# Emission by a list scheduler with a time model in an eight-core decoder trunk

## The chip, the cores and the metric

The kernel runs on the eight cores of one Trainium2 chip (two dies: cores 0 to 3 and 4 to 7). Each core computes one sequence of the batch; the cores don't exchange data. The metric is the device time of the slowest core in microseconds (us). In the lines of the profile, PE is TensorE (PEld its weight loads), DVE is VectorE, ACT is ScalarE and POOL is GpSimd. A PSUM bank is one of the eight buffers of `ps_all` (128 x 8 x 512 in the kernel) that TensorE writes its results to; the program has it written again only when DVE or ACT has read it (gate/up stood 104 us for that in the kernel before). GLA is gated linear attention.

Executions come in two states. In the slow one the cores of a die, or of both, are granted a lower TensorE clock for long stretches. Even a fast run can hold a short stretch at 0.81 of the clock on some cores, so beside the time of a run I use its **undisturbed cores**: those whose clock records in the profiled run hold no 0.81 at all. Three chips served the experiments, called A, B and C here. Cores of the kernel before that ran at a mean clock of at least 0.944 had medians of 6857, 6849 and 6837 us on them, so up to 20 us between kernels can be the chip; where that matters, I say which chip it was.

## The reference

```python
# x: (8, 4096, 1024) float32.  D_MODEL 1024, D_FF 2816
def rms_norm(x, g):
    return x * rsqrt(mean(x * x, -1) + 1e-6) * g
def swiglu_ffn(h, w_in, w_down):
    gate, up = split(h @ w_in, 2)
    return (silu(gate) * up) @ w_down

for i in range(2):                     # layer 0: GLA, layer 1: differential attention
    x = x + 0.5 * swiglu_ffn(rms_norm(x, g), w_in, w_down)      # FFN 0 / FFN 2
    x = x + mixer[i](rms_norm(x, g))
    x = x + 0.5 * swiglu_ffn(rms_norm(x, g), w_in, w_down)      # FFN 1 / FFN 3
return rms_norm(x, final_norm)
# mixer 0: gated linear attention, chunks of 64, 4 heads (projection, "core", output projection)
# mixer 1: (softmax(Q1 K1^T) - lam * softmax(Q2 K2^T)) V, causal, 8 heads, two 64-wide maps each
# ... cut
```

A core works through eight tiles of 512 tokens; each passes all of both layers. Keys and values of earlier tiles are kept in device memory, so attention grows from tile 0 to tile 7.

## The kernel before

A program in Python writes out each engine's instructions in a fixed order; the engines then run in that order and wait on semaphores. The trace shows one order whatever the times: in the profiled run before, ACT's 3826 and DVE's 4435 records have the same sequence on all eight cores, and TensorE's 37152 on the six cores that hold that many. The kernel before decides the order with generators that yield a cost. Two of them, attention and a chain of dense tasks, are woven by how far each has come:

```python
db["list"] = [0, 1] if lim else [0, 1, 2, 3]          # PSUM banks of the dense work
gens = [[chain(x), 0.0, max(1e-6, sum(tk.cost for tk in x)), bool(x)] for x in (lt, dn)]
while any(g[3] for g in gens):
    live = [g for g in gens if g[3]]
    g = min(live, key=lambda g: g[1] / g[2])           # the one least far along
    try:
        g[1] += next(g[0])
    except StopIteration:
        g[3] = False
```

What follows a matmul group (evacuation, norm) is emitted at once. The norm that ends a projection holds its transposes back by one row block only:

```python
class NormPipe:
    # ... cut
    def done(self, s, of):             # after the x update of row block s, half `of`
        stat_half(p, s, of)            # ACT: square with row sums
        if of == 1:
            stat_rstd(p, s)            # POOL: 1/sqrt
            i = norm_hb(p, s)          # DVE: x * rstd, bf16
            self.pump()                # PE: transposes of the row block before
            self.pend = (p, s, i, self.n_idx)
# ... cut
```

The key tiles go through two staging buffers to device memory, and attention issues one chunk of scores at a time, the values two chunks behind:

```python
def k_cons(c, b):
    i = c % 2
    k.op(DVE, lambda: nc.vector.tensor_copy(out=kst[i][:], in_=bank[b][:]), ...)
    # ... cut
    k.dma(SP, t_kc[c, t], t_kst[i], [(kvc[c, t, :, 0:512], kst[i][:])])
# ... cut
for n in range(N + LAG):               # LAG = 2
    if n < N:
        qk(n)                          # 4 matmuls of 64 rows, two at once; then exp on ACT
    if n >= LAG:
        pv(n - LAG)                    # 8 matmuls of 128 rows x 129 columns
    # ... cut
```

The softmax here doesn't subtract the row's maximum and nothing guards it: scores larger than these inputs give would overflow.

## Time and profile before

| | before |
|---|---|
| time | 6953.8 us, median of three (6903.14 to 7202.15) |
| profiled run, slowest core | 7143.8 us, with one stretch of 2300 to 2600 us, most of it at clock 0.81, on every core |
| undisturbed execution, stitched from two cores | 6860 us |
| TensorE useful work at measured spacing | 5441 us |

The lines are in the prediction below. Two habits of reading matter: "busy" counts slow matmuls as busy, so useful work is columns times the measured spacing (0.2158 us for 512 columns; at full clock starts on core 2 are 0.109 us apart for 256 columns, 0.056 to 0.057 for 129 and 0.056 for 128, and 64-row matmuls that go two at once start 3 to 4 ns apart); and a wait listed as "PE L412 <- DVE L403" is time in which TensorE stood at a transpose until the DVE had written its input.

### The profile page before, as it was taken

What the parts mean: (1) busy time and instruction counts of PE and PEld (TensorE: products, weight loads), DVE (VectorE), ACT (ScalarE), POOL (GpSimd) and SP (SyncE); (2) the same over time, 40 slices, a digit from 0 to 9 for tenths busy, and PEclk for the clock granted to TensorE, in tenths of its full rate; (3) what the DMA queues carried; (4) which work ended last, traced back from release to release, by engine and by line L of the source; (5) the groups of instructions that cost most, each with busy time, mean ns of one, the idle gap of its engine ahead of it and who ended that gap; (6) DMA issues with size and microseconds to landing.
All of it is one profiled execution on the core that took longest, in us unless ns stands there. A gap on an engine that the chain in (4) does not pass through costs nothing.

```text
span 7143.8 us, 103951 instructions; the slowest of 8 cores (7062.5 to 7143.8 us)
## 1 busy us (share of the span) xinstructions
PE 6330.8 (89%) x37152; PEld 2987.2 (42%) x37152; DVE 2530.7 (35%) x4435; ACT 2179.2 (31%) x3826; POOL 534.3 (7%) x1294
## 2 busy tenths in 40 slices
PE   6887679987899879998999879999899999899889
PEld 2343234443444434443444434444444444344454
DVE  2432254334433443234433343322433222433113
ACT  1211221133113421253114531155311355211681
POOL 1111021001000010000000010000000000000000
PEclk9898789998999989998999999987788887788777
DMA  9689757442345324443445324443243443234432
GB/s 211 168 178 211 177 128 221 142 147 95 130 157 164 114 93 171 157 131 101 152 141 166 121 93 153 160 146 107 83 139 120 139 119 116 85 121 129 142 102 86
DMA packets 331317, 984.58 MB, mean 138 GB/s; under 512 B 38447, under 2 KB 55232, under 8 KB 330816
## 3 DMA queue, kind: packets, MB, share of 16 engines
q1 hardware_dynamic: 306432, 891.88, 39.0%
q0 software_dynamic: 24384, 86.04, 8.1%
q8 instruction: 311, 5.10, 0.3%
q14 instruction: 190, 1.56, 0.1%
HBM read 944.11 MB, written 119.70 MB: 149 GB/s over the span
## 4 chain that ended last, share of the span: by engine, by line
PE 72%; DMA 8%; DVE 8%; issue 4%; ACT 4%; POOL 3%; SPq 1%; DVEq 0%; ACTq 0%; POOLq 0%
PE ps_all L503 31%; PE ps_all L580 16%; PE ps_all L995 8%; PE ps_all L630 6%; PE ps_all L966 5%; PE ps_all L608 4%; DMA sb_wring<-wpack 3%; DMA wscr<-sb_wring 3%; PE ps_all L412 1%; DVE sb_hT L419 1%; SPq L172 1%; ACT sb_junk L384 1%; DMA kvc<-sb_work 1%; ACT sb_junk L829 1%; DVE sb_work L835 1%
## 5 line engine op out<-in xcount | busy, mean ns | idle before, releaser
L503 PE MATMUL ps_all<-sb_hT,sb_wring 128*128 128x512 bf16 (+1 forms) x11584 | 2750.2, 395 | 172.8 <-DVE sb_work L517 104.2
L503 PEld LDWEIGHTS ps_all<-sb_hT,sb_wring 128*128 128x128 bf16 x11584 | 1150.0, 102 | 1530.1 <-issue 712.4
L580 PE MATMUL ps_all<-sb_wring,sb_work 128*128 128x512 bf16 x5632 | 1375.9, 403 | 74.3 <-DMA sb_wring<-wpack 53.8
L971 ACT ACTIVATE sb_work<-ps_all 128x1024 bf16<-128x1024 f32 (+1 forms) x1088 | 1071.9, 996 | 801.4 <-PE ps_all L966 783.2
L509 ACT ACTIVATE sb_th<-ps_all 128x512 f32<-128x512 f32 x704 | 419.8, 596 | 1988.9 <-PE ps_all L503 1986.0
L511 DVE SCALAR_TENSOR_TENSOR sb_tg<-sb_th,ps_all 128x512 f32<-128x512 f32 x704 | 483.3, 686 | 1240.2 <-ACT sb_th L509 1239.8
L580 PEld LDWEIGHTS ps_all<-sb_wring,sb_work 128*128 128x128 bf16 x5632 | 564.3, 102 | 759.4 <-issue 337.4
L995 PE MATMUL ps_all<-sb_work 128*128 128x129 bf16 x8448 | 735.6, 236 | 20.1 <-DVE sb_work L1007 19.4
L384 ACT ACTIVATE sb_junk<-sb_xt 128x512 bf16<-128x512 f32 x448 | 281.8, 629 | 1497.9 <-DVE sb_xt L589 1150.6
L630 PE MATMUL ps_all<-sb_wring,sb_hT 128*128 128x512 bf16 x2560 | 653.3, 405 | 45.7 <-DVE sb_hT L419 12.7
L995 PEld LDWEIGHTS ps_all<-sb_work 128*128 128x128 bf16 x8448 | 533.4, 104 | 280.4 <-issue 278.2
L517 DVE TENSOR_TENSOR sb_work<-ps_all,sb_tg 128x512 bf16<-128x512 f32 x704 | 486.1, 690 | 396.9 <-PE ps_all L503 384.8
L966 PE MATMUL ps_all<-sb_work 64*128 64x256 bf16 (+1 forms) x4352 | 461.3, 294 | 92.1 <-DMA sb_work<-kvc 65.2
L589 DVE SCALAR_TENSOR_TENSOR sb_xt<-ps_all,sb_xt 128x512 f32<-128x512 f32 x256 | 176.9, 691 | 752.3 <-PE ps_all L580 750.6
L608 PE MATMUL ps_all<-sb_hT,sb_wring 128*128 128x512 bf16 x1536 | 385.9, 406 | 40.4 <-DVE sb_work L899 30.1
L630 PEld LDWEIGHTS ps_all<-sb_wring,sb_hT 128*128 128x128 bf16 x2560 | 251.9, 103 | 339.5 <-issue 167.5
L966 PEld LDWEIGHTS ps_all<-sb_work 64*128 64x128 bf16 x4352 | 127.8, 95 | 519.7 <-issue 492.3
L412 PE MATMUL ps_all<-sb_ident,sb_hb 128*128 128x128 bf16 x1536 | 131.9, 236 | 221.6 <-DVE sb_hb L403 200.1
L403 DVE TENSOR_SCALAR sb_hb<-sb_xt,sb_rstd 128x1024 bf16<-128x1024 f32 x192 | 144.6, 753 | 470.4 <-POOL sb_rstd L391 470.4
L395 POOL TENSOR_TENSOR sb_ssq<-sb_ssq 128x1 f32<-128x1 f32 x224 | 48.5, 216 | 2801.1 <-ACT sb_junk L384 2801.0
L419 DVE TENSOR_TENSOR sb_hT<-ps_all,sb_norms 128x1024 bf16<-128x1024 bf16 x192 | 233.7, 1219 | 67.6 <-PE ps_all L412 66.1
L608 PEld LDWEIGHTS ps_all<-sb_hT,sb_wring 128*128 128x128 bf16 x1536 | 153.8, 103 | 228.0 <-issue 116.8
(88 smaller groups left out, 2595.4 us busy)
## 6 DMA issues: line engine op xcount, KB each, us to landing
sb_wring<-wscr SPq DMA_DIRECT2D x1120, 512.0 KB, 4.2
sb_work<-kvc SPq DMA_DIRECT2D x576, 258.0 KB, 2.9
sb_wring<-wpack POOLq DMA_DIRECT2D x160, 512.0 KB, 23.3
wscr<-sb_wring SPq DMA_DIRECT2D x160, 512.0 KB, 12.4
sb_xt<-x SPq DMA_DIRECT2D x32, 512.0 KB, 4.7
out<-sb_xt SPq DMA_DIRECT2D x32, 512.0 KB, 3.3
sb_wring<-wscr SPq DMA_DIRECT2D x56, 256.0 KB, 2.9
kvc<-sb_work SPq DMA_DIRECT2D x64, 130.0 KB, 3.1
```

What stands on the lines that cost most here:

```text
L384: k.op(ACT, lambda: nc.scalar.activation(out=junk[:], in_=xt[:, p, s, of * 512:(of + 1) * 512], func=AF.Square, accum_out=ssq[:, p, s, of: ...
L419: k.op(DVE, lambda: nc.vector.tensor_tensor(out=dst, in0=pt[:, :, :], in1=norms[:, n_idx, :].unsqueeze(2).to_broadcast([128, KC, 128]), op ...
L503: k.op(PE, lambda: nc.tensor.matmul(bank[b][:, lo:lo + n], lhsT=w[:, kc, u * 128:(u + 1) * 128], rhs=hT[:, p, kc, lo:lo + n], start=(kc == ...
L509: k.op(ACT, lambda: nc.scalar.activation(out=th[q][:], in_=bank[b][:], func=AF.Tanh, scale=0.5), reads=[t_bank[b]], writes=[t_th[q], t_ban ...
L511: k.op(DVE, lambda: nc.vector.scalar_tensor_tensor(out=tg[q][:], in0=th[q][:], scalar=1.0, in1=bank[b][:], op0=ALU.add, op1=ALU.mult), rea ...
L517: k.op(DVE, lambda: nc.vector.tensor_tensor(out=act[:, c, :], in0=bank[b][:], in1=tg[q][:], op=ALU.mult), reads=[t_tg[q], t_bank[b]], writ ...
L580: k.op(PE, lambda: nc.tensor.matmul(bank[b][:], lhsT=act[:, c, s * 128:(s + 1) * 128], rhs=wring[i][:, (c % 4) * 512:(c % 4 + 1) * 512], s ...
L608: k.op(PE, lambda: nc.tensor.matmul(bank[b][:], lhsT=w[:, kc, cc * 128:(cc + 1) * 128], rhs=hT[:, p, kc, :], start=(kc == 0), stop=(kc == ...
L630: k.op(PE, lambda: nc.tensor.matmul(bank[b][:], lhsT=hT[:, p, kc, s * 128:(s + 1) * 128], rhs=wring[i][:, (kc % 4) * 512:(kc % 4 + 1) * 51 ...
L966: k.op(PE, lambda: nc.tensor.matmul(psall[:, b0 + m, kk * 256:kk * 256 + w], lhsT=lhs, rhs=qT[m * 64:(m + 1) * 64, h, qs:qs + w], start=Tr ...
L971: k.op(ACT, lambda: nc.scalar.activation(out=pT[pi][:, :, 0:ncol], in_=psall[:, b0:b0 + 2, 0:ncol], func=AF.Exp, scale=0.125), reads=[t_ba ...
L995: k.op(PE, lambda: nc.tensor.matmul(obv[j][:, m, 0:129], lhsT=pT[pi][:, m, c0:c0 + 128], rhs=v, start=(it["first"] and kk == 0 and m == 0) ...
```

## The change

Its intent: order the work by when its inputs are due, so that a matmul whose input is late doesn't stand at the head of TensorE's queue. Every operation gets a modelled duration and every tile a modelled due time. Tasks and their follow-up chains are coroutines that say what they need next.

```diff
+    def op(self, eng, fn, reads=(), writes=(), inc=True):
+        dur, lat = self._cost(eng, ins)       # ACT: 0.2 + n * 0.0008, 0.1
+        at = eng.free                         # ... max with the due times of reads and writes
+        eng.free = at + dur
...
+    def schedule():
+        while running or sides or waiting:
+            start_tasks()
+            now = PE.free
+            run_sides(now + 0.25)             # chains on ACT, DVE, POOL, SP that are due
+            cands = [...]                     # PE steps: chains first, then tasks by key
+            ok = [c for c in cands if c[0] <= now + 0.05]
+            c = min(ok, key=lambda c: c[1]) if ok else ...   # else whatever is due first
...
+    def free_banks():
+        return [b for b in sorted(pool) if b not in held]    # up to 8 PSUM banks
...
-        for n in range(N + LAG):
-            if n < N:
-                qk(n)
+        for n in range(0, N + LAG, step):     # step 2; 1 in the last tile
+                for m in cur_n:
+                    qk(m)
...
+        task(f"core_{u}", ..., [f"gproj_{u}"] + ([f"att_{u - 1}"] if u else []), -500.0, ...)
+        task(f"down3_{t}", lambda t=t, g=spare: ffn_down(t, 3, final_block(t), not g),
+             [f"~gu3_{t}"], B + (3.2 if spare else 1.6), B + (4.0 if spare else 2.6), 38)
```

The last line is the **filler**: the last down projection of a tile has a key that spreads it over the next tile's FFNs; it then goes out in groups of four matmuls, with four banks held. (Cuts are marked with "..." and the bodies are shortened.)

## The prediction

> **What bounds the kernel now.** I read the page first: its span, engine shares and slices.
>
> ```profile
> span 7143.8 us, 103951 instructions; the slowest of 8 cores (7062.5 to 7143.8 us)
> PE 6330.8 (89%) x37152; PEld 2987.2 (42%) x37152; DVE 2530.7 (35%) x4435; ACT 2179.2 (31%) x3826; POOL 534.3 (7%) x1294
> PEclk9898789998999989998999999987788887788777
> DMA  9689757442345324443445324443243443234432
> ```
>
> TensorE (PE) is busy 89% and no other engine passes 35%, so PE sets the time. But busy is not useful work. In order of time, the chain that ended last holds unbroken stretches of one line:
>
> ```profile
> 1949.65 63.02 PE ps_all L503 x292
> 5470.37 67.22 PE ps_all L503 x256
> ```
>
> The first is 63.02/292 = 0.2158 us per 512-column matmul, the second 0.2626. The granted clock says why. The windows view of core 2 gives 1.00 in 4400-4600 us and 0.81 in 5200-5400 us. In the trace the clock takes three values: 1, 0.81 and 0.5. The 0.81 state fills one stretch of 2300 to 2600 us on every core, but early on cores 0, 1, 4 and 5 and late on the others. So I build an undisturbed execution from two halves: core 2 up to the start of tile 5's attention at 4657 us, then core 4 from the same point (4864) to its end (7067). Sum 4657 + 2203 = **6860 us**. The fastest timed run, 6903 us, is close, so timed runs are nearly free of the 0.81 state and I predict in these undisturbed microseconds.
>
> **Useful work.** From the groups by form at the measured spacing: 20,672 full matmuls x 0.2158 = 4461 us. [...]8448 PV matmuls of 129 columns 475; 4352 QK matmuls, two at once in half the rows, 230; transposes and GLA about 275. Sum 5441 us. So 6860 - 5441 = **1419 us** are lost, and this is what the change can win. The waits of PE name part of it (core 2):
>
> ```profile
> PE ps_all L412 <- DVE sb_hb L403: 200.1, 51, 35.8
> PE ps_all L503 <- DVE sb_work L517: 104.2, 51, 4.3
> PE ps_all L412 <- DVE sb_work L1035: 77.5, 16, 7.0
> PE ps_all L966 <- DMA sb_work<-kvc: 65.2, 8, 23.0
> PE ps_all L580 <- DMA sb_wring<-wpack: 53.8, 18, 4.7
> ```
>
> The first is the norm chain at the end of each projection (x update, square, rstd on POOL, scale, then the transpose): PE has nothing else queued. The second is a wait for a PSUM bank, of which dense work has only four, or two beside attention. All such waits sum to about 800 us. The next two lines (timeline of core 4 in pure attention) show another loss:
>
> ```profile
> 6801.19 0.39 PE L966 MATMUL ps_all<-sb_work 64*128 64x256 bf16 x4
> 6801.52 0.63 PE L995 MATMUL ps_all<-sb_work 128*128 128x129 bf16 x8
> 6802.09 0.39 PE L966 MATMUL ps_all<-sb_work 64*128 64x256 bf16 x4
> ```
>
> One iteration is 0.90 us where its columns need 0.67. From single starts in the trace, each change between 64-row and 128-row matmuls costs about 0.095 us over normal spacing, 0.19 per iteration; x1088 iterations = 207 us. Finally the clock falls to 0.5 after idle stretches (some 750 us of core 2 are spent there), which costs some 200 us of slow matmuls; it goes when the idle stretches go. 800 + 207 + 200 is 1207; the remaining 210 are short gaps and the start.
>
> [...]
>
> **The change part by part.**
>
> 1. No arithmetic changes. The order listing has the same matmuls but for the split of first chunks (384+128 columns, before 256+256). Useful work stays 5441.
>
> 2. Attention in pairs (step 2; 1 in the last tile). I counted runs of 64-row matmuls in the order listing: 1086 before, 667 after. 419 x 0.19 = **80 us saved**.
>
> 3. Norm chains, evacuations and group transposes become side chains, emitted when the model says that their input is due; dense work of another task stands in between. In the listing, tile t's last down projection now stands in groups of four matmuls among the up projections of tile t+1, and the norm transposes stand singly between other matmuls. Up to eight banks serve instead of four. This addresses the 800 us of waits and most of the 200 us at half clock. What cannot be filled: the first pass and the last tile.
>
> 4. First pass. Windows of core 2:
>
> ```profile
> 0.00:849.00 849.00, 633.37 (x3004) 290.12 (x3004) 263.25 (x403) 129.82 (x280) 112.58 (x244) 0.90 0.88 194
> 849.00:953.00 104.00, 73.36 (x458) 32.23 (x458) 65.93 (x177) 45.02 (x101) 17.55 (x35) 0.81 0.48 122
> ```
>
> DMA is 88% busy: every weight is read in float32, cast, stored and later reread. In its full stretches about 20 slots arrive per 100 us, 4.9 us each, against 3.45 us of matmuls per slot (16 x 0.2158). The order and the ring of 12 slots are the same, so the change can only close the pieces where DMA isn't full: some 40 us where tile 1's first FFN runs, and 25 of the 104 us of the first attention. I take 953 -> **890 us**.
>
> 5. The rest, before 6860 - 953 = 5907 us. Useful work in it 5441 - 630 = 4811 (630 lies in the first 953 us). Mode changes (667 - 24) x 0.19 = 122. Residual: in the densest slice before (4400-4600 us of core 2) the same count of columns gives 196 us of useful work in 200; attention mixed with projections will not hold that, and model and chip differ, so I choose 3.5% of 4811, 170 us. The end, output projection, FFN and final norm of the last tile, has no filler: about 30 us, as now. Sum 5133.
>
> 890 + 5133 = 6023. The limiter and run-to-run spread were 43 to 94 us above the stitched 6860 in the two fast runs; [...]I add 20: **6045 us**, 13% less than 6953.8.
>
> **The rivals.**
>
> A. A wait takes the place of the removed one. Order is frozen at build time from a time model, and queues are in order. If DVE or ACT run late against it, PE stands at a head-of-line wait as before. For: the model takes 0.61 us for the square, the trace 0.63 plus 0.19 for its accumulator read; ACT table loads (1.28 us each, 16 before) may grow with tanh and ln closer together; rstd shares POOL's queue with weight loads in the first pass. Against: its other durations match the rows (exp 1.02, hT 1.22, DVE 0.69 us), and PE is slightly slower than modelled, which gives the others slack. If half of the 800 us of waits come back: about 6400.
>
> B. ACT becomes the bound in the last attention. Exponentials there start every 0.903 us in the trace, so 248 take 224 us and squares some 16 more. PE needs 163 + 47 + 45 of filler = 255. Nearly balanced: at most 20 us lost, inside my range.
>
> C. Denser PE draws the 0.81 clock over the whole span. For: the early cores were in it for their first 2500 us. Against: dense stretches at clock 1.00 run for 200 us with no fall. Cost if it held half of the span: stitched from the throttled halves, before would be 7144 instead of 6860, so some 280 more, about 6320; such a run is called slow.
>
> D. DMA: steady slices are 40 to 50% busy, so 13% less time leaves room. No bound.
>
> **Range and chances.** The residual sets the range: 1% to 6.5% of 4811 is -120 to +145; the first pass is uncertain by 40, the limiter by 50. I take 5900 to 6230. To come within 2% nearly all of the removed waits would have to return: 0.02; slower 0.01; faster 0.97.
>
> **What would show it.** Right: waits of PE on the norm scale under 60 us in sum; bank waits of the gate/up line under 40; under 300 us at clock 0.5; start to start of 64-row runs in pairs; stages between attentions falling from 510 to about 450 us at clock 1; the first attention over near 890 us. Wrong if PE waits in sum stay above 350 us, if the last attention is still over 280 us with the filler inside it, or if the 0.81 state covers most cores' spans in the fast runs.

## The result

All outputs were correct. The changed kernel took **6223.6 us**, median of four (6199.3, 6205.9, 6241.3 and a slow 7028.8); the kernel before, in the same rounds, 7003.7 us, median of four (6903.1 to 7202.2). The ratio of fast runs is 0.897 (95% interval 0.886 to 0.908), so the change is faster by 10%. A ratio is the mean time of one kernel's fast runs over that of the other's of the same rounds, so not quite the ratio of these medians. The forecast was 13% and 6045 us; the direction was right, the size was not. The fast runs have a mean of 6215 us, inside the stated range only at its upper end.

The head of the profile page after:

```profile
span 6197.9 us, 103483 instructions; the slowest of 8 cores (6154.1 to 6197.9 us)
...
PE 5712.1 (92%) x36586; PEld 2907.6 (47%) x37216; DVE 2512.6 (41%) x4435; ACT 2120.1 (34%) x3826; POOL 530.9 (9%) x1070
...
PEclk9998979999999999999999999998999999999999
DMA  9879967664345634465344753555534565345652
```

TensorE is busy 92% against 89%, with some 600 us less busy time (5733 on core 2, where it was 6331): the long stretch at 0.81 is gone from this run (one of 160 us remains on cores 0, 1, 6 and 7), and the slow matmuls after idle stretches are fewer: core 2 spent 315 us at clock 0.5, before 756. Of the stretches at 0.5 on core 2, 36 of 38 had TensorE idle for 1 us or more on end in the 5 us before they began (105 of 108 in the kernel before); of all moments, taken 1 us apart, 9% had (before 19%). Cores 2 to 5 are undisturbed: 6154 to 6168 us, median 6163.6, which is what the prediction's 6023 stands against.

TensorE's waits on core 2 after (columns: us in total, times, longest):

```profile
PE ps_all L619 <- DVE sb_hb L646: 80.5, 29, 35.5
PE ps_all L807 <- DMA sb_wring<-wpack: 61.5, 21, 3.7
PE ps_all L880 <- DVE sb_work L1246: 42.7, 1, 42.7
PE ps_all L619 <- DVE sb_work L1129: 41.4, 15, 5.0
PE ps_all L732 <- DVE sb_work L1246: 39.0, 8, 10.3
...
PE ps_all L732 <- DVE sb_work L751: 5.9, 8, 1.3
```

L619 is the transpose (before L412), L646 the norm scale (L403), L732 gate/up (L503), L751 its evacuation (L517), L1246 the copy of a key tile to its staging buffer (L899), L1129 the output of the GLA core (L835). All waits sum to 415 us, before 804. The norm scale fell from 200 to 80, and of these 80 some 66 lie in the first pass (36 before the first matmul, as in the kernel before). After the first pass it fell from 122 to 14:

```profile
PE ps_all L619 <- DVE sb_hb L646: 14.2, 18, 1.7
```

Gate/up's wait for a bank fell from 104 to 6. But the key copy, which had held TensorE for 30 us (at L608), now holds it for 82, 43 of them at once in the first pass: a wait that I had counted among the removed ones grew.

The windows of core 2 (length, then busy time and instructions of PE, PEld, DVE, ACT, POOL, then the clock, DMA share and GB/s), cut at the end of the first attention, at the last attention's start and at its end:

```profile
0.00:901.00 901.00, 687.77 (x3470) 318.59 (x3472) 323.53 (x569) 172.08 (x375) 127.22 (x249) 0.91 0.88 192
901.00:5729.00 4828.00, 4647.07 (x29936) 2356.39 (x29936) 2068.21 (x3617) 1675.76 (x3069) 373.47 (x765) 0.99 0.51 156
5729.00:6009.00 280.00, 261.77 (x3122) 158.06 (x3121) 64.02 (x166) 245.04 (x323) 17.89 (x38) 0.99 0.54 153
```

I then counted for each interval between two matmul starts of this core its useful part (columns at the measured spacing), 0.095 us for each change between 64 and 128 rows (a 64-row matmul starts 0.312 us after a 512-column one and not 0.216, and a 128-row one 0.202 us after a 64-row one of 256 columns and not 0.109), the extra time at clock 0.5 (0.427 us from start to start for 512 columns), and the rest as idle:

| core 2 after, us | 0 to 901 | 901 to 5729 | 5729 to 6009 | to the end |
|---|---|---|---|---|
| useful | 628 | 4482 | 202 | 131 |
| mode changes | 2 | 78 | 47 | 0 |
| half clock | 38 | 38 | 1 | 3 |
| idle | 197 | 231 | 30 | 7 |

The start and the last instructions add 35 and 13. After the first pass, half clock and idle are 269 us in the middle and 31 in the last attention: **300 where the prediction chose 170**.

The pairs are there, and a run of eight 64-row matmuls (core 4) takes one entry and one exit:

```profile
5294.52 0.61 PE L1326 MATMUL ps_all<-sb_work 64*128 64x256 bf16 x8
5295.06 1.08 PE L1361 MATMUL ps_all<-sb_work 128*128 128x129 bf16 x16
```

And this is the key copy at work (timeline of core 2: start, length, engine, line; in brackets the idle time before it and who ended it):

```profile
4953.15 1.89 PE L732 MATMUL ps_all<-sb_hT,sb_wring 128*128 128x512 bf16 x8 [0.62 <-DVE sb_hT L629]
...
4958.86 1.29 DVE L1246 CAST sb_work<-ps_all 128x512 bf16<-128x512 f32 x2 [5.85 <-DMA kvc<-sb_work]
...
4962.85 0.69 DVE L1246 CAST sb_work<-ps_all 128x512 bf16<-128x512 f32 x1 [2.71 <-DMA kvc<-sb_work]
...
4964.47 0.69 DVE L1246 CAST sb_work<-ps_all 128x512 bf16<-128x512 f32 x1 [0.92 <-DMA kvc<-sb_work]
...
4965.31 3.15 PE L732 MATMUL ps_all<-sb_hT,sb_wring 128*128 128x512 bf16 x7 [10.27 <-DVE sb_work L1246]
```

The DVE stands at three copies in turn, each waiting for the store of an earlier key tile to leave one of two buffers. It stands 5.85, 2.71 and 0.92 us. Behind them in its queue is the gate's evacuation, and the copies hold PSUM banks. TensorE has dense work of another task at hand, as I had predicted, but no bank to put it in: it stands for 10.27 us.

### The profile page after: what moved, and what is told of

It is laid out like the page before. It is cut to its first block, busy times and chain, and to the rows that moved or that the text cites.

```text
span 6197.9 us, 103483 instructions; the slowest of 8 cores (6154.1 to 6197.9 us)
## 1 busy us (share of the span) xinstructions
PE 5712.1 (92%) x36586; PEld 2907.6 (47%) x37216; DVE 2512.6 (41%) x4435; ACT 2120.1 (34%) x3826; POOL 530.9 (9%) x1070
## 4 chain that ended last, share of the span: by engine, by line
PE 79%; DMA 9%; DVE 5%; issue 3%; ACT 2%; POOL 1%; SPq 1%; DVEq 0%; ACTq 0%; POOLq 0%
PE ps_all L732 36%; PE ps_all L807 17%; PE ps_all L1361 8%; PE ps_all L880 7%; PE ps_all L1326 4%; DMA sb_wring<-wpack 4%; PE ps_all L860 3%; DMA kvc<-sb_work 2%; PE ps_all L619 2%; DMA wscr<-sb_wring 2%; ACT sb_work L1331 1%; DMA sb_xt<-x 1%; DVE sb_hT L629 1%; DVE sb_work L1374 1%; SPq L222 1%
## 5 line engine op out<-in xcount | busy, mean ns | idle before, releaser
L732 PE MATMUL ps_all<-sb_hT,sb_wring 128*128 128x512 bf16 (+2 forms) x11344 | 2543.5, 376 | 110.7 <-DVE sb_work L1246 51.3
L732 PEld LDWEIGHTS ps_all<-sb_hT,sb_wring 128*128 128x128 bf16 x11648 | 1112.8, 99 | 1366.6 <-issue 192.7
L807 PE MATMUL ps_all<-sb_wring,sb_work 128*128 128x512 bf16 x5443 | 1289.4, 384 | 75.2 <-DMA sb_wring<-wpack 60.9
L1331 ACT ACTIVATE sb_work<-ps_all 128x1024 bf16<-128x1024 f32 (+1 forms) x1088 | 1019.5, 1000 | 389.8 <-PE ps_all L1326 387.3
L880 PE MATMUL ps_all<-sb_wring,sb_hT 128*128 128x512 bf16 x2467 | 605.9, 387 | 79.3 <-DVE sb_work L1246 44.4
L1361 PE MATMUL ps_all<-sb_work 128*128 128x129 bf16 x8448 | 633.0, 222 | 12.5 <-DVE sb_work L1374 9.7
L751 DVE TENSOR_TENSOR sb_work<-ps_all,sb_tg 128x512 bf16<-128x512 f32 x704 | 486.4, 691 | 363.4 <-PE ps_all L732 317.5
L1326 PE MATMUL ps_all<-sb_work 64*128 64x256 bf16 (+1 forms) x4352 | 356.5, 272 | 23.3 <-ACT sb_work L1331 18.3
L860 PE MATMUL ps_all<-sb_hT,sb_wring 128*128 128x512 bf16 x1492 | 349.1, 380 | 13.3 <-DVE sb_hT L629 7.4
L610 POOL TENSOR_SCALAR sb_ssq<-sb_ssq 128x1 f32<-128x1 f32 x224 | 87.0, 388 | 2685.6 <-ACT sb_junk L600 2685.0
L1326 PEld LDWEIGHTS ps_all<-sb_work 64*128 64x128 bf16 x4352 | 159.7, 95 | 227.0 <-issue 186.4
L860 PEld LDWEIGHTS ps_all<-sb_hT,sb_wring 128*128 128x128 bf16 x1536 | 146.6, 98 | 183.2 <-issue 21.4
L646 DVE TENSOR_SCALAR sb_hb<-sb_xt,sb_rstd 128x1024 bf16<-128x1024 f32 x192 | 143.9, 751 | 213.7 <-POOL sb_rstd L613 213.5
L619 PE MATMUL ps_all<-sb_ident,sb_hb 128*128 128x128 bf16 x1536 | 123.4, 227 | 80.2 <-DVE sb_hb L646 80.0
```

What stands on the lines that cost most here:

```text
L732: k.op(PE, lambda: nc.tensor.matmul(bank[b][:, lo:lo + n], lhsT=w[:, kc, u * 128:(u + 1) * 128], rhs=hT[:, p, kc, lo:lo + n], start=(kc == ...
L751: k.op(DVE, lambda: nc.vector.tensor_tensor(out=act[:, c, :], in0=bank[bu][:], in1=tg[r][:], op=ALU.mult), reads=[t_tg[r], t_bank[bu]], wr ...
L807: k.op(PE, lambda: nc.tensor.matmul(bank[b][:], lhsT=act[:, c, s * 128:(s + 1) * 128], rhs=wring[i][:, (c % 4) * 512:(c % 4 + 1) * 512], s ...
L860: k.op(PE, lambda: nc.tensor.matmul(bank[b][:], lhsT=w[:, kc, cc * 128:(cc + 1) * 128], rhs=hT[:, p, kc, :], start=(kc == 0), stop=(kc == ...
L880: k.op(PE, lambda: nc.tensor.matmul(bank[b][:], lhsT=hT[:, p, kc, s * 128:(s + 1) * 128], rhs=wring[i][:, (kc % 4) * 512:(kc % 4 + 1) * 51 ...
L1326: k.op(PE, lambda: nc.tensor.matmul(psall[:, b0 + m, kk * 256:kk * 256 + w], lhsT=lhs, rhs=qT[m * 64:(m + 1) * 64, h, qs:qs + w], start=Tr ...
```

## The experiments

Fifteen kernels ran, all correct; four of them (r1 to r4) put kernels that had run before side by side on one chip. "Clean" is the median of the undisturbed cores in the profiled run. For r1 and r4, whose profiled runs were slow, it is that of the four cores of the undisturbed die (clock at least 0.973) in a timed run; for r2 and r3 that of all cores at 0.975 and above in all their runs.

| run | edit to the changed kernel | chip | clean, us | difference |
|---|---|---|---|---|
| e1_kst8 | eight key buffers | A | 6093.8 | -70 |
| e2_core_late | GLA core after the output projection | A | 6141.8 | -22 |
| e6_actcost | model's ACT cost | A | 6155.1 | -9 |
| e9_all | these three | A | 6075.0 | -89 |
| e3_step1 | no pairs | B | 6219.5 | +56 |
| e4_nofill | no filler | B | 6101.4 | -62 |
| e8_bank4 | four banks | B | 6219.2 | +56 |
| e5_nomodel | time model off | B | none | 8246 to 8544, all slow |
| e10_all_nofill | e9 and no filler | C | 6039.9 | -124 |
| e11_last_pairs | pairs in the last tile | C | 6156.6 | -7 |
| e7_before_pairs | the kernel before, pairs alone | C | 6805.4 | -32 to -50 of before |
| r1_after | none | A | 6159.7 | base of the next three |
| r2_all | as e9 | A | 6081.8 | -78 |
| r3_all_nofill | as e10 | A | 6060.3 | -99 |
| r4_nofill | as e4 | A | 6116.8 | -43 |

Differences of the upper block are from 6163.6, which was measured on a chip that the record doesn't name; r1 measured 6159.7 for the same kernel on chip A. Those of the last three are from r1. An edit changes what the time model sees, and so the order of much else than what it aims at; the waits that it was not meant to move have to be looked at too. The same kernels were 11 us (e4) and 20 us (e10) faster on B and C than on A, so differences found on B and C lean that far to the low side.

### Where the 130 us went: three suspected waits

My theory after the result: the missing gain lies in named waits that the scheduler makes or leaves. The rival: it is spread as a slack of every stage, because model and chip differ.

**e1_kst8** gives the key tiles eight buffers, so that no copy waits for a store.

```diff
-        kst = [carve(R_ACT + i * 1024, 1024, BF16) for i in range(2)]
+        kst = [carve(R_ACT + i * 1024, 1024, BF16) for i in range(8)]
-        vo = R_ACT + 2048
+        vo = R_ACT + 8192
-            i = c % 2
+            i = c
```
(and the same for their semaphores and flags)

> Eight buffers for the key tiles on their way to HBM, where the changed kernel has two; nothing else. Theory A (named waits cause the shortfall): the copies into two buffers stand at the head of VectorE's queue until the store of the one before has landed (15 us from issue to landing), and hold the evacuations behind them; TensorE waits 82 us in all for that copy on a core that never left full clock (43 of them once, in the first pass). With eight buffers these waits go below 10 us and the shortest core span falls from 6147-6156 to 6070-6090 us. Theory B (the residual is general mismatch of model and chip; a named wait that is removed comes back elsewhere, for instance as the wait of the first attention for its key blocks): the waits on that copy go, others grow, and the gain is under 25 us.

Measured: 6085 to 6105 us on eight undisturbed cores, 70 less; the profiled run took 6105.68 us. Its other timed runs were slow, so there is no ratio. The waits on the key copy are gone from the list; two others on core 4 took a part of it, where the changed kernel's core 2 shows 20.9 and 10.4:

```profile
PE ps_all L1326 <- ACT sb_work L1331: 35.5, 55, 6.6
PE ps_all L1361 <- DVE sb_work L1374: 28.0, 21, 3.2
```

By place (medians of the undisturbed cores) it looks different. The first pass, where 43 us of waits went, became only 5 us shorter (896 to 891) and took on 9 us more of useful work; other waits grew there, the one in the second line to 17.0. The stretch from the end of the first attention to the start of the last became 63 us shorter (4835 to 4771). On core 4, where it lost 67, its idle time fell by 51, as much as its waits on the key copy (50.8); 7 were at half clock, and 8 are useful work that moved to the first pass. So theory A holds after the first pass, and in it theory B for about half. The order had changed as well: the attentions of tiles 1 to 6 took 94 us less and the stretches between them 31 more.

A reading to put right: the page's row of 130-KB stores (15.0 us from issue to landing, before 3.1) is that of the value tiles. The key tiles' are the 128-KB ones, 5.4 us on core 2 against 3.8 before. With two buffers it is the number of them, not a slow store, that makes the copies wait.

**e2_core_late** holds the GLA core back until the output projection of the tile before it has been finished, so that two norm chains don't fall together.

```diff
-    [f"gproj_{u}"] + ([f"att_{u - 1}"] if u else [])
+    [f"gproj_{u}"] + ([f"att_{u - 1}", f"dout_{u - 1}"] if u else [])
```

> The GLA core of the next tile starts only when the output projection of the attention and its norm chain are done, so that the core's gaps can be filled with the gate and up projection. Theory A: the 15 waits of up to 5 us for the core's gated output (41 us in all) come from two chains on VectorE and ScalarE at the same time with no filler left; started later, they fall below 15 us and the shortest span falls by 20 to 40 us. Theory B: the bubble moves to the norm chain of the output projection (waits for the scaled rows, 80 us now, grow by as much) and the time stays within 10 us.

Measured: 6138 to 6146 us, 22 less; ratio to before 0.887 (0.860 to 0.913). The wait fell from 41 to 24 us, but another grew from 6 by as much:

```profile
PE ps_all L732 <- DVE sb_tg L743: 23.6, 15, 8.8
PE ps_all L619 <- DVE sb_work L1129: 23.5, 9, 5.8
```

The stage ahead of the last attention became 12 us longer (432 against 420), since the last core has nothing to be held behind. A wait that the edit does not aim at moved too: gate/up's on the key copy fell from 48 to 24 us (medians of undisturbed cores). In e6 below the same two waits moved by the same amounts (48 to 23 and 6 to 24), and the stretch between the first attention and the last stayed at 4836 us, so the two about cancel. What is left for e2 is the core's wait: 18 us less, against 16 by which that stretch became shorter (4835 to 4819).

**e6_actcost** corrects the model's cost of the scalar engine: an exponential occupies the engine for 0.90 us, its spacing in the trace, instead of 1.02, with the difference put into its latency.

```diff
-            return 0.2 + n * 0.0008, 0.1
+            return 0.085 + n * 0.0008, 0.215
```

> Only the time model is edited: an exponential of 1024 elements advances ScalarE by 0.904 us, as they start back to back in the trace, in place of 1.02. Theory: in the last attention the model thinks ScalarE the bound, hands all filler to the first half (TensorE-bound, 40 exponentials per 50 us) and leaves the second half ScalarE-bound without filler (49 to 51 per 50 us). With the right cost filler spreads further, the last attention falls from 279 to 262-270 us and the whole by 10 to 20. Rival: order hardly moves, no change beyond 10 us.

Measured: 6155.1 us, 9 less; ratio 0.887 (0.862 to 0.913). Nearly all of it lies in the last attention, 268 us against 278 to 280. A wrong duration in the model cost 9 us, all of it in that stage. No other duration of the model was varied, so this doesn't measure the rival that model and chip differ everywhere.

**e9_all** joins the three edits.

> The three edits of e1, e2 and e6 together. If each removes its own wait the gains add: shortest span 6000 to 6050 us. If a common limit stands behind them (theory B), no better than the best single one by more than 10 us.

Measured: 6066 to 6091 us on six undisturbed cores, 89 less, of a sum of 100 for the three; 78 when it was repeated beside its base (r2). Against e1 the last attention is 10 us shorter, and the stretch between the first and the last only 9 (4771 to 4762): on top of the key buffers, holding the core back is worth about 9 us and not 22. Ratio to before 0.880 (0.865 to 0.895), times 6096.8 to 6124.4 us in its three fast runs.

### The parts of the change

**e3_step1** undoes the pairs.

```diff
-             attention(t, 1 if t == NTL - 1 else 2)
+             attention(t, 1)
```

> Undoes one part alone: attention issues score and value matmuls one chunk at a time in all tiles, not in pairs. Theory A (each change between 64-row and 128-row matmuls costs 0.095 us of TensorE): about 420 more runs of 64-row matmuls, so +80 us on cores with no 0.81 stretch, 6163 to about 6240. Rival B (that loss lies beside waits for the exponential, which single chunks shorten or lengthen): clearly other than +80, namely under +30 or over +130. The two last-tile stages (279 us) must not change, because the last tile has single chunks already.

Measured: 6207 to 6226 us, 56 more; runs of 64-row matmuls rose from 667 to 1080. The trace of both kernels shows the entry at 0.312 us after a 512-column matmul and the exit as before, so each of 413 runs still costs 0.19 us, 78 in sum. On core 6 the table of intervals gives 205 us of mode changes against 127, and idle time 20 to 30 us lower than on the changed kernel's undisturbed cores, once the 139 us of useful work are put back whose records this trace lacks. The theory's cost was right, and about a quarter of it was hidden: waits that pairs lengthen (L1326 for the exponential, 20 us in pairs, 11 without) are paid back.

**e7_before_pairs** puts pairs alone into the kernel before.

```diff
-            if n < N:
-                qk(n)
+            if n % 2 == 0:
+                for m in (n, n + 1):
+                    if m < N:
+                        qk(m)
```
(with one key/value buffer fewer and one probability buffer more)

> The kernel before with one part of the change alone: score matmuls go out in pairs of chunks (one key/value buffer fewer, one probability buffer more); everything else as before. Runs of 64-row matmuls fall from 1086 to 543. Theory A (0.19 us for each run removed, none of it given back): 543 x 0.19 = 103 us less, undisturbed cores from about 6850 to about 6747. Rival B (part is given back by waits for exponentials and key/value buffers, as in the changed kernel, where 413 runs gave 40 to 60 us and not 78): 40 to 75 us less, 6775 to 6810.

Measured: 0.993 of the time before (0.989 to 0.997), which is 50 us; cores at a clock of at least 0.944 on this chip had medians of 6797 and 6837 us, 40 less (32 with the four undisturbed cores of the profiled run). The rival was right: of 103 us of mode changes about half came back, in waits for the exponential (core 1; before 26.4 on core 2):

```profile
PE ps_all L412 <- DVE sb_hb L403: 198.9, 51, 34.5
...
PE ps_all L966 <- ACT sb_work L971: 60.5, 99, 2.1
```

The norm scale's 199 us stay, so they need the scheduler.

**e8_bank4** holds the bank pool to the first four banks.

```diff
-        return [b for b in sorted(pool) if b not in held]
+        return [b for b in sorted(pool) if b not in held and b < 4]
```

> Undoes one part alone: the bank pool is held to the first four banks where it had up to eight. Theory A (bank waits of gate/up, 104 us before and 6 us after, went because of the wider pool): those waits return, 60 to 100 us in sum, undisturbed cores 6163 to 6225-6265. Rival B (they went because the follow-ups are emitted when due, which frees banks early): bank waits stay under 25 us and the time within 20 us of 6163.

The profiled run was slow on die 0 alone; cores 4 to 7 are undisturbed and took 6214 to 6223 us, 56 more. The lines (core 5) show that neither theory had it:

```profile
PE ps_all L860 <- DVE sb_work L1246: 84.5, 20, 17.3
PE ps_all L732 <- DVE sb_hT L629: 38.4, 22, 2.8
PE ps_all L732 <- DVE sb_work L751: 3.8, 6, 1.0
```

Gate/up's bank wait does not come back (3.8), so it was not the pool that removed it; the order of emission is what remains; with the model off (e5) and eight banks it is 24 on core 5. The wider pool pays elsewhere: for the key projection (L860), whose banks wait for the staging buffers, and for norm transposes.

**e4_nofill** lets the last down projection go out at once in all tiles but the last but one, whose filler goes into the last attention.

```diff
-             B + (3.2 if spare else 1.6), B + (4.0 if spare else 2.6), 38)
+             B + (3.2 if spare else 1.57), B + (4.0 if spare else 1.59), 38)
```

> Takes the filler away: the last down projection of a tile goes out at once when its gate/up is done, not in groups of four spread through the next stage. Theory A (the filler is what covers the norm chains and the exponential): waits for the norm scale and for the transposed norm copy grow by 2 to 4 us per tile and half, and the last attention loses the 39 us inside it but the stage before it gets them; in sum +30 to +100 us on undisturbed cores, 6163 to 6195-6260. Rival B (side chains alone cover them, since dense work of another task is always at hand): within 20 us of 6163.

Measured: 6092 to 6108 us on die 1, 62 less; its faster fast run took 6136.6 us. Both theories were wrong: I had expected it slower, or the same. Waits of core 4:

```profile
PE ps_all L619 <- DVE sb_hb L646: 73.0, 22, 34.8
...
PE ps_all L732 <- DVE sb_work L1246: 10.1, 5, 3.3
```

The norm scale's wait is no longer without the filler, so the filler isn't what covers it. The key copy's wait at gate/up fell from 53 (core 5 of the changed kernel; 39 on core 2) to 10. That fits the four banks that the filler holds through those stages, though no run here held the banks by themselves, and e2 and e6, which leave the filler as it is, halve the same wait.

**e10_all_nofill** is e9 without the filler.

> All four corrections together: eight key staging buffers, the GLA core task held back until the previous output projection has been emitted, the corrected cost of the scalar engine in the model, and no filler between tiles. Theory A (the filler cost its 60 us only by pulling the key-tile copies into the store's shadow, which eight buffers already cure): within 15 us of the three corrections alone, 6065 to 6090 on undisturbed cores. Rival B (the filler costs by itself, by keeping 16 weight slots and the next tile's work waiting): another 40 to 60 us less, 6015 to 6040.

Measured: 6029 to 6048 us on all eight cores, 35 less than e9, but on another chip. It is the best version: its one fast run took **6049.0 us**, against 6199 to 6241 for the changed kernel and 6865 to 6905 for before on this chip. Five further runs had one die slow (6313 to 6873 us), with the other die's cores at 6030 to 6083.

```profile
span 6048.0 us, 105162 instructions; the slowest of 8 cores (6028.7 to 6048.0 us)
...
PE 5717.2 (95%) x37568; PEld 2915.4 (48%) x37568; DVE 2512.9 (42%) x4435; ACT 2118.4 (35%) x3826; POOL 517.6 (9%) x1070
...
PEclk9998879999999999999999999999999999899999
```

Core 4's waits sum to 316 us, of which 76 are the norm scale and 58 the float32 weights of the first pass. Its half clock and idle time after the first pass are 217 us, against 310 by the same count for core 2 of the changed kernel.

**r1 to r4** settle how much of this was the chip. No edits are new; the four kernels ran one after the other on chip A.

> The changed kernel again, as the base for the three others on the same chip. Its undisturbed cores were at 6154 to 6168 us on another chip; on the chip of the last runs the same instructions up to the last attention took some 25 us less. So 6135 to 6170 here, and the differences of the other three are taken from this run.

> The three edits (key buffers, core held back, cost of the scalar engine), filler kept, on the same chip as the changed kernel: 75 to 100 us less than it on undisturbed cores.

> The same without the filler. Theory A (with eight key buffers the filler costs nothing more; the 35 us between the earlier runs were mostly the chip): within 15 us of the three edits with filler. Rival B (the filler costs by itself): 25 to 45 us less.

> The changed kernel without the filler, on the same chip. Theory A (the 62 us were the filler): 50 to 70 us less than the changed kernel. Rival B (a third or more of them was the chip): 25 to 45 us less.

Measured: without the filler the changed kernel gained **43 us** (6159.7 to 6116.8), so a third of the 62 had been the chip or chance. With the three edits the filler still costs **22 us** (6081.8 to 6060.3), between the two theories. Stage by stage on core 4 of r2 and r3, from the first attention's end to the last one's start, it is 4759 against 4733 us. So the filler is a loss in both settings, about half of it through what the three edits cure. Its fast run took 6094.6 us, that of r2 6098.7. r3 also has a spread: in its fast run cores 0, 1, 4 and 5 took 6046 to 6059 us and cores 2, 3, 6 and 7 took 6088 to 6094, with no more 0.81 in their clocks and the same 0.2158 us per matmul. The trace names most of it. First core 2, then core 4:

```profile
PE ps_all L1326 <- DMA sb_work<-kvc: 44.6, 8, 7.7
```
```profile
PE ps_all L1326 <- DMA sb_work<-kvc: 13.9, 7, 4.5
```

Between the first attention and the last (915 to 5624 us), TensorE waited 27 to 32 us for key and value blocks on cores 2, 3, 6 and 7, and at most 5.3 on the other four; that stretch differs by some 40 us between the two groups. Why the blocks came late on those cores alone is not shown. The 22 us rest on the median of both groups; on cores 0, 1, 4 and 5 of the fast run alone they would be about 30.

**e5_nomodel** switches the model off: everything is due at once. Tasks, banks, pairs and filler stay.

```diff
-        dur, lat = self._cost(eng, ins)
+        dur, lat = 1e-6, 0.0
```
(and the same for transfers)

> Switches the time model off: every operation and transfer is taken to be done at once, so each chain and its follow-up goes out as soon as its order allows, while tasks, eight banks, pairs, side chains and filler stay. Theory A (the due times carry the gain): head-of-line waits on the norm scale, the tanh and the weights come back, 6163 to 6300-6550 on undisturbed cores. Rival B (structure carries it: banks, pairs and filler): under +60, below 6225.

Measured: 8246 to 8544 us, all four runs slow, so it can't be held against fast runs to the microsecond. If the 4069 us that core 5 (8472 us) spent at 0.81 had all run at full clock, at most 0.19 x 4069 = 773 would go, which leaves 7700: slower than before by far more than the effect I look for. Page and waits of core 4:

```profile
PE 6888.1 (81%) x37440; PEld 3304.8 (39%) x37440; DVE 2548.8 (30%) x4435; ACT 2136.0 (25%) x3826; POOL 515.2 (6%) x1070
...
PEclk9888789886989888776777777777767777677777
```
```profile
PE ps_all L618 <- DVE sb_hb L645: 857.3, 192, 64.1
```

(Lines are shifted by one.) Each of the 192 norm transposes is now emitted straight after its chain, and TensorE stands 4.5 us at each. The scheduler without its model is worse than the old weave, which at least held transposes back by a row block. So without its due times the rest of the scheduler is a loss, and the filler carries none of the gain. As the edit takes all due times away at once, it doesn't say which use of them gains how much.

### The last attention

**e11_last_pairs** uses pairs in the last tile as well.

```diff
-             attention(t, 1 if t == NTL - 1 else 2)
+             attention(t, 2)
```

> The changed kernel with pairs in the last tile too, where it has single chunks: 123 runs of 64-row matmuls fewer. Theory A (the exponential sets the last attention, 274 of its 279 us on the scalar engine): its stage stays at 279 us within 5 us, though 23 us of mode changes are gone. Rival B (TensorE sets it): 255 to 262 us.

Measured: the stage took 294 to 297 us, not 279 nor 260. Neither theory holds. The 274 us in my expectation added up records of exponentials that overlap (back to back on core 2 of the changed kernel, with records of 1.02 us, they most often started 0.920 us apart, or 0.903); in the windows the scalar engine is busy 245 of 278 us, and TensorE 261. Neither is full; they hand work to and fro. Waits of core 4 inside the stage, with pairs:

```profile
PE ps_all L1326 <- ACT sb_work L1331: 34.0, 64, 1.8
ACT sb_work L1331 <- PE ps_all L1326: 33.5, 57, 2.5
```

and in the changed kernel with single chunks:

```profile
ACT sb_work L1331 <- PE ps_all L1326: 21.9, 37, 2.3
```

A pair needs both score slots, so it can start only when the second exponential has read its banks, and then the scalar engine stands until the scores are there. Single chunks pay 23 us more of mode changes and still win here. The total (6149 to 6163 us on six cores) is not higher, because everything up to the last attention, the same instructions, took 20 to 35 us less on chip C than in the profiled run of the changed kernel.

## Why the prediction was wrong

**What held.** Useful work: 5443 us counted from the trace against 5441. Mode changes: 667 runs, 127 us. First pass: 901 us on core 2 (889 to 898 on the other undisturbed cores) against 890. Gate/up's bank waits under 40: 6. The undisturbed 6860 of before: 6837 to 6857 on chips A, B and C. Rivals C and D didn't come: no fast run was mostly at 0.81, and e10 runs shorter than the changed kernel with the same tensors to move (984.6 MB in the traces of before, the changed kernel, e1, e4 and e5). What brings the 0.81 clock is not shown: e10 was at 95% busy on its slowest core with a mean clock of 0.978 to 0.980 on all eight, e5 at 81% with 0.789 to 0.797 in its profiled run.

**The step that failed** is in part 5, "so I choose 3.5% of 4811, 170 us". It was a choice from the densest slice of before, not a count of waits, and it measured 300: 130 of the 140 us between the predicted 6023 and the measured 6163.6. The other 11 are the first pass. The second, smaller miss is the term for limiter and spread, "I add 20", an estimate that no run measured: the fast runs' mean of 6215 lies 52 above the undisturbed cores.

**What stands in its place.** Part 3 argued that "in the listing" dense work stands between a norm chain and its transposes. That was true and not enough: a listing shows what comes next, not which buffers it still needs. Key copies with two buffers (70 us, of which 63 after the first pass), two norm chains at once (22 alone, about 9 on top of the key buffers), a wrong duration of the exponential (9) and the filler (43 alone, 22 on top of the others) are the named terms. On one chip all four together are worth 99 us of the 130 and bring the kernel to 6060; on chip C it ran at 6040, 17 above the predicted 6023. Some 30 us stay without a name. Rival A was right in kind: waits took the place of those removed. But they were staging buffers and what the filler holds up, which I hadn't listed, and not the square or the table loads that I named (of these a core has 17, before and after).

**The gain of pairs** (80 us) was right as a cost and too high as a gain: 56 in e3 (some 10 more if chip B's lead is added), 32 to 50 in e7.

**The other signs.** Norm-scale waits 80 (I said under 60; 36 of them are the wait before the first matmul, which is in the 200 of before as well), 315 us at clock 0.5 on core 2 (under 300), stages between attentions 472 to 483 on core 2 (450), waits in sum 415 (over 350, which I had named as the sign of a wrong prediction). In the last attention (278 to 280) rival B's balance held, with a loss of 9 us by e6. One reading of the prediction to put right: the 7144 us under rival C are core 2 as it ran and nothing stitched (its two throttled parts would give 4864 + 2487 = 7351).

**Open.** Why the filler costs 22 us once the key buffers are cured was not tested; the four banks that it holds are a guess. The 188 us of idle time in e10 after the first pass are spread over many kinds of waits, none of them over 20 us. Why key and value blocks came late on four cores of r3 is unexplained.

## What to carry to other kernels

A forecast of "waits that will be filled" needs a second question for each: which buffer or PSUM bank does the filling work need, and who holds it then? Size the residual from those waits, not as a percentage. And take away each part of a scheduler once it runs: here nothing of the gain was left without due times, and the filler, a headline part, was a loss. An edit to such a scheduler changes its whole order, so compare all waits and stages and not the one aimed at: of the key buffers' waits about half came back in the first pass and none after it.
